# Issuing the DMAs of a hybrid layer's background sums from GpSimd instead of SyncE

## The chip, the cores and the metric

The kernel runs on one core of a Trainium2 chip, in one launch. The core has five engines with queues of their own: TensorE (PE: matmuls; PEld: its weight loads), VectorE (DVE), ScalarE (ACT), GpSimd (POOL) and SyncE (SP). Each queue is worked off in order, and an instruction that waits for a semaphore holds everything behind it on its engine. The metric is the device time of one execution in microseconds (us). A profiled execution gives the trace from which all rows below are taken.

## The reference, cut to what matters

The layer works on x with 2048 tokens and 1024 channels, in float32. Its first half (a state-space scan and a windowed attention, side by side) ends in x2, the residual stream. The second half is the MLP, with 4096 hidden channels:

```
x = x + rmsnorm(mix, norm_mix_post)                 # x2, 1024 x 2048
h = rmsnorm(x, norm_mlp_pre)
f = jnp.square(jax.nn.relu(h @ w_up)) @ w_down
x = x + rmsnorm(f, norm_mlp_post)
```

The row factor of the MLP's first rmsnorm is a scalar per token, so the kernel leaves it out of h and applies its square at the end (`drr` holds it); what enters the MLP is x2 times the weight vector.

## The kernel before

**The MLP's products.** `up` and `down_fast` use a seven-product scheme (Strassen's, in a form with running sums): a 2x2 block product is made with seven matmul products of sums and differences of blocks instead of eight. Each product needs a left factor made of blocks of weights and a right factor made of blocks of activations. Every factor is split into a high and a low part (fp32r), and three matmuls per k tile stand for one float32 product: 12 matmuls of 128x512 per product.

**Stages.** `main` runs the MLP's first layer for the token halves `hf` 0 and 1, each in 16 steps `p` (`up`), and then the second layer (`down_fast`, `down`). One step `p` is seven products in the order `PROD` = 1, 5, 6, 3, 7, 2, 4. Products share three PSUM banks (psmx, psmy, psmz), and a bank must be read before the next product adds to it: ACT copies products 1, 5 and 6 out (tiles c1, c5, c6; L1120) and reads product 4 with the relu (c4, L1073); DVE adds products 3, 7 and 2 to c6, c5, c1 (L1123). ACT then takes relu and square (L1073, L1074). The c tiles and sums of them (t1, t2, t4 on DVE, L1083 to L1095) are stored to DRAM as `dop` (L1079). The ring of c tiles has 5 buffers.

**Weights.** `up_weights` loads four blocks per step (`wu`, L982, 256 KB each, 8 buffers), forms sums on DVE (L964) and splits them (`wsplit`: ACT L969, DVE L970).

**Side work.** Generators (`side`) are stepped by a clock that counts matmul time, and a scheduler then places each engine's instructions by the time at which it expects them to be ready; only PE's order is kept as written. Around the change run:

- `sums` (from step `p` = 4 of the first half on): the background sums. 20 jobs. Jobs 0 to 3 load four blocks of x2 (L1158), scale them on DVE (L1167), form four differences on POOL (L1169 to L1172) and store seven tiles as `dxo` (L1185). Jobs 4 to 19 load four blocks of `w_down` (L1160), make four sums on POOL in place (L1179) and store them as `dws` (L1187). The four loaded tiles `sum` come from a ring of 4 buffers with the tag `nt`, which a job fills entirely; t1, t2, t4 come from rings of 3 and 2 buffers that `up` and the loads named stg use too.
- `r2`: the row factor of the rmsnorm, once per half at `p` = 8, for two token blocks. `rnorm` takes three tiles of the same `nt` ring (rn_v, rs_y, rs_t; ACT L282 and L284, DVE L283 to L288) and stores `drr` (L1338).
- `up_input1` (steps 14 and 15 of the first half): loads the 28 `dxo` tiles (`stage`, L199) and splits them (ACT L1012, DVE L1013) as the second half's right factors.
- `down_input` (steps 14 on of the second half as written; its first loads are placed some steps earlier): loads `dop` tiles (L199) and splits them (ACT L1246, DVE L1247).
- `down_weights`: its first four loads `wd` (L1218) use the `nt` ring again, after the last job's tiles. Later loads `wd` from `dws` (L1227) use another ring.

So in the kernel before, all of these loads and stores stand in SP's queue: weights, `dop`, stg, `drr`, and the background sums' 80 loads and 92 stores, each of 256 KB. The tiles of a job, and who gets the buffers next, tie POOL, SP, ACT and DVE together:

```
t = a[f"{i + 1}{k + 1}"] = self.nt("sum")
...
r = (x_sums if len(job) == 1 else w_sums)(*job, a)
...
raw = [self.nt("wd").rearrange("p (k c) -> p k c", k=4) for _ in range(2)]
```

Of the kernel before, what the change touches and what calls it, by code (L numbers as in the profile page):

```python
# [38 lines left out]
class Layer:  # L39
# [1105 lines left out]
    def sums(self):  # L1145


        nc = self.nc
        vec = self.vec["norm_mlp_pre"]

        def load(job):
            a = {}
            for i in range(2):
                for k in range(2):
                    t = a[f"{i + 1}{k + 1}"] = self.nt("sum")
                    if len(job) == 1:
                        kt = 4 * i + job[0]
                        nc.sync.dma_start(t, self.d_x2[kt, :, self.tok(1, k)])  # L1158
                    else:
                        nc.sync.dma_start(t.rearrange("p (k c) -> p k c", k=4),  # L1160
                                          self.a["w_down"][2 * job[1] + i, 2 * job[0] + k])
            return a

        def x_sums(i, a):
            for y in ("11", "12", "22", "21"):
                kt = 4 * int(y[0]) - 4 + i
                nc.vector.tensor_scalar(a[y], a[y], vec[:, kt:kt + 1], None, ALU.mult)  # L1167
            t1, t2, t4 = self.ld(name="t1"), self.gl("t2"), self.ld(name="t4")
            nc.gpsimd.tensor_sub(t1, a["12"], a["11"])  # L1169
            nc.gpsimd.tensor_sub(t2, a["22"], t1)  # L1170
            nc.gpsimd.tensor_sub(a["12"], a["22"], a["12"])
            nc.gpsimd.tensor_sub(t4, a["21"], t2)  # L1172
            return {1: a["11"], 3: a["22"], 2: a["21"], 5: t1, 6: t2, 7: a["12"], 4: t4}

        def w_sums(qt, p, a):
            r = {}
            for m, fn, x, y, o in ((5, "tensor_add", "21", "22", "21"), (6, "tensor_sub", "21", "11", "11"),
                                   (7, "tensor_sub", "22", "11", "22"), (3, "tensor_sub", "12", "11", "12")):
                getattr(nc.gpsimd, fn)(a[o], a[x], a[y])  # L1179
                r[m] = a[o]  # L1180
            return r

        def store(m, job, a):
            if len(job) == 1:
                nc.sync.dma_start(self.d_xo[m - 1, job[0]], a)  # L1185
            else:
                nc.sync.dma_start(self.d_ws[(5, 6, 7, 3).index(m), job[0], job[1]], a)  # L1187
        jobs = [(i,) for i in range(4)] + [(qt, p) for qt in range(4) for p in range(4)]
        for n, job in enumerate(jobs):
            a = load(job)  # L1190
            yield 10
            r = (x_sums if len(job) == 1 else w_sums)(*job, a)
            yield 8
            for m, t in r.items():
                store(m, job, t)
            if n == 3:
                self.flags.add("xo")
            elif n > 3 and job[1] == 3:
                self.flags.add(f"sum{job[0]}")
            yield 5  # L1200
# [462 lines left out]
```

## Time and profile before

| | us |
|---|---|
| median of 3 runs (3203.62 to 3218.38) | 3213.89 |
| the profiled execution, its own time | 3205.63 |
| its span in the trace | 3203.8 |
| PE busy in the span | 2949.0 (92%) |
| DVE busy | 2196.2 (69%) |
| ACT busy | 1554.0 (49%) |
| POOL busy | 903.7 (28%) |
| first background load issued / last background store issued | 1940.0 / 2465.2 |

PE is the engine that runs nearly all the time, and it is idle or slow only where one of the others is late. The background sums run from 1940 to 2470 us of the span. The rows of that stretch stand in the section after the next: busy time per stretch of time, the chain of waits, the timeline of single engines, the waits of SP's queue, and the groups of instructions of a line. A row of the timeline names in brackets how long the engine was idle before it and what ended that.

### The profile page before, as it was taken

The page shows a single profiled execution, that of the slowest core. Times are in us where ns is not written, and L with a number is a line of the kernel's source. Part 1 is how long each engine was busy: PE and PEld are TensorE (multiplying, and loading weights), DVE is VectorE, ACT ScalarE, POOL GpSimd, SP SyncE. Part 2 cuts the span into 40 slices and gives each one's busy share as a digit, 9 for nine tenths or more (in the row PEclk, how much of TensorE's full clock was granted, in tenths as well). Part 3 has the DMA queues.
Part 4 walks back from the last instruction along what each step waited for, and adds up shares of the span by engine and source line. Part 5 has one row for each costly group of instructions (what it writes and reads, how often), then busy time and mean ns, then how long its engine had stood idle before and what let it go on. Part 6 is the DMA issues. An engine that isn't in the chain of part 4 may idle for free. (4 is left out here: it accounts for less than half of the span.)

```text
span 3203.8 us, 41029 instructions
## 1 busy us (share of the span) xinstructions
PE 2949.0 (92%) x13560; PEld 2358.2 (74%) x13560; DVE 2196.2 (69%) x3671; ACT 1554.0 (49%) x2886; POOL 903.7 (28%) x743
## 2 busy tenths in 40 slices
PE   7989999989999899898897878998998999998996
PEld 6778887878886576576575657776887888877886
DVE  7355555547756778867868867677767567776765
ACT  4234566567765545322223354656565644454432
POOL 4242222112224344555545522141203000020001
PEclk9999999999999999899898989999999999999998
DMA  6767544465567755556436458778647565557633
GB/s 228 238 205 198 155 130 119 122 203 156 138 192 241 238 143 163 164 181 187 119 101 221 165 189 274 243 257 279 239 165 271 193 207 192 189 188 222 229 98 97
DMA packets 430213, 603.87 MB, mean 188 GB/s; under 512 B 35632, under 2 KB 203568, under 8 KB 430000
## 3 DMA queue, kind: packets, MB, share of 16 engines
q1 hardware_dynamic: 395376, 565.58, 57.0%
q10 hardware_dynamic: 34624, 35.66, 3.2%
q8 instruction: 108, 1.77, 0.2%
q14 instruction: 105, 0.86, 0.1%
HBM read 399.11 MB, written 201.99 MB: 188 GB/s over the span
## 5 line engine op out<-in xcount | busy, mean ns | idle before, releaser
L90 PE MATMUL psg<-h,ws 128*128 128x512 f32 x1920 | 486.6, 400 | 19.7 <-ACT z L474 17.9
L90 PEld LDWEIGHTS psg<-h,ws 128*128 128x128 f32 x1920 | 356.9, 190 | 93.4 <-issue 18.6
L88 PE MATMUL psmx<-b,ws 128*128 128x512 f32 x1152 | 297.0, 409 | 46.8 <-ACT c L1120 20.5
L222 POOL TENSOR_SCALAR ws<-wr 128x512 fp32r<-128x512 f32 x184 | 126.2, 686 | 755.9 <-PE psg L90 617.4
L88 PEld LDWEIGHTS psmx<-b,ws 128*128 128x128 f32 x1152 | 226.6, 198 | 102.3 <-ACT c L1120 22.4
L225 POOL TENSOR_TENSOR ws<-wr,ws 128x512 fp32r<-128x512 f32 x184 | 249.4, 1356 | 14.8
L90 PE MATMUL psg<-hr,ws 128*128 128x512 f32 x960 | 248.7, 400 | 4.0 <-DMA hr<-dh 3.3
L781 DVE CUSTOM_DVE_ANT_0 p<-psqk,pack,sinks 128x384 f32<-128x384 f32 (+1 forms) x256 | 151.9, 596 | 138.2 <-PE psqk L90 137.5
L90 PE MATMUL psg<-ga,ws 128*128 128x512 f32 x768 | 208.7, 424 | 28.9 <-DVE mix L897 14.2
L88 PE MATMUL psx<-ff,ws 128*128 128x512 f32 x1008 | 231.6, 390 | 0.0
L88 PEld LDWEIGHTS psx<-ff,ws 128*128 128x128 f32 x1008 | 189.2, 188 | 40.0 <-issue 0.5
L90 PE MATMUL psg<-ya,ws 128*128 128x512 f32 x768 | 213.0, 418 | 3.5 <-DVE ya L205 3.3
L969 ACT CAST ws<-wd 128x512 fp32r<-128x512 f32 x196 | 121.4, 622 | 177.6 <-PE psx L88 75.7
L90 PEld LDWEIGHTS psg<-ga,ws 128*128 128x128 f32 x768 | 149.4, 199 | 77.6 <-issue 13.6
L90 PEld LDWEIGHTS psg<-hr,ws 128*128 128x128 f32 x960 | 176.0, 189 | 40.8 <-DMA hr<-dh 6.1
L1179 POOL TENSOR_TENSOR sum<-sum 128x512 f32<-128x512 f32 x64 | 97.8, 1538 | 326.6 <-DMA sum<-w_down_dram 182.2
L90 PEld LDWEIGHTS psg<-ya,ws 128*128 128x128 f32 x768 | 142.0, 193 | 44.9 <-issue 15.1
L792 ACT ACTIVATE p<-p,m 128x384 f32<-128x384 f32 (+1 forms) x256 | 150.9, 591 | 37.4 <-DVE m L787 37.2
L90 PE MATMUL psy<-ff,ws 128*128 128x512 f32 x672 | 159.2, 394 | 7.2 <-DVE facc L1288 6.0
L210 ACT CAST pt<-pspt 128x512 fp32r<-128x512 f32 x184 | 107.0, 583 | 118.8 <-PE pspt L94 104.8
L970 DVE TENSOR_TENSOR ws<-wd,ws 128x512 fp32r<-128x512 f32 x196 | 137.7, 703 | 31.4 <-ACT ws L969 31.1
L211 DVE TENSOR_TENSOR pt<-pspt,pt 128x512 fp32r<-128x512 f32 x184 | 125.4, 683 | 49.2 <-ACT pt L210 48.8
(250 smaller groups left out, 6279.1 us busy)
## 6 DMA issues: line engine op xcount, KB each, us to landing
stg<-dop SPq DMA_DIRECT2D x196, 256.0 KB, 3.6
wu<-w_up_dram SPq DMA_DIRECT2D x128, 256.0 KB, 3.7
wr<-w_in_dram SPq DMA_DIRECT2D x120, 256.0 KB, 2.8
dop<-c SPq DMA_DIRECT2D x112, 256.0 KB, 3.4
wd<-dws SPq DMA_DIRECT2D x56, 512.0 KB, 4.2
k<-dk SPq DMA_DIRECT2D x56, 384.0 KB, 4.8
dop<-t SPq DMA_DIRECT2D x84, 256.0 KB, 3.5
wd<-w_down_dram SPq DMA_DIRECT2D x40, 512.0 KB, 4.7
```

The costliest lines, as they stand in the source:

```text
L88: self.nc.tensor.matmul(out, lhsT, rhs, start=False, stop=stop, skip_group_check=True)
L90: self.nc.tensor.matmul(out, lhsT, rhs, start=start, stop=stop)
L210: self.nc.scalar.copy(hi, src)
L211: self.nc.vector.tensor_sub(lo, src, hi.bitcast(F32))
L222: self.nc.gpsimd.tensor_scalar(w[:, 0], raw, 1.0, 0.0, ALU.mult, ALU.add)
L225: eng.tensor_sub(w[:, 1], raw, w[:, 0].bitcast(F32))
L781: nc.vector.tensor_tensor_reduce(out=p[:, :W], in0=ps[:, :W], in1=bias, scale=1.0, scalar=self.sinks[:, hd:hd + 1], op0=ALU.add, op1=ALU.m ...
L792: nc.scalar.activation(p4[r][:, :W], p4[r][:, :W], AF.Exp, bias=m[:, 0, r:r + 1], scale=float(np.float32(SLOPES[hd])), accum_out=m[:, 2, r ...
L969: self.nc.scalar.copy(w[:, 0], x)
L970: self.eng("wlo").tensor_sub(w[:, 1], x, w[:, 0].bitcast(F32))
L1179: getattr(nc.gpsimd, fn)(a[o], a[x], a[y])
```

## The change

The four `dma_start` calls of the background sums, two loads and two stores, are begun from GpSimd's queue. The tiles, the sums and their order in the program stay.

```
@@ load @@
-                        nc.sync.dma_start(t, self.d_x2[kt, :, self.tok(1, k)])
+                        nc.gpsimd.dma_start(t, self.d_x2[kt, :, self.tok(1, k)])
...
-                        nc.sync.dma_start(t.rearrange("p (k c) -> p k c", k=4),
+                        nc.gpsimd.dma_start(t.rearrange("p (k c) -> p k c", k=4),
                                           self.a["w_down"][2 * job[1] + i, 2 * job[0] + k])
@@ store @@
-                nc.sync.dma_start(self.d_xo[m - 1, job[0]], a)
+                nc.gpsimd.dma_start(self.d_xo[m - 1, job[0]], a)
...
-                nc.sync.dma_start(self.d_ws[(5, 6, 7, 3).index(m), job[0], job[1]], a)
+                nc.gpsimd.dma_start(self.d_ws[(5, 6, 7, 3).index(m), job[0], job[1]], a)
```

PE's order stays the same. On the other engines it moves, since the scheduler places the work anew. Five pieces follow; the numbers behind c and t name one buffer's use, so that a place can be found again.

POOL, one job of `w_down` in the changed kernel. Before, POOL's queue held in this stretch only the sums L1179, 64 in a row.

```order
L1160 DMA sum<-w_down_dram 128x512 x4
L1179 TENSOR_TENSOR sum<-sum 128x512 x2
L1187 DMA dws<-sum 128x512
L1179 TENSOR_TENSOR sum<-sum 128x512 x2
L1187 DMA dws<-sum 128x512 x3
```

The loads and stores of a job now stand between its sums, and the next job's loads behind its last store.

SP, steps 13 and 14 of the first half, where `up_input1` begins (dop is a store of `up`, wu a load of weights, stg<-dxo a load of `up_input1` further on); one piece of the difference.

```order
 L1079 DMA dop<-t_18716 128x512
-L982 DMA wu<-w_up_dram 128x512
-L1187 DMA dws<-sum 128x512 x3
-L982 DMA wu<-w_up_dram 128x512
-L1160 DMA sum<-w_down_dram 128x512 x4
+L982 DMA wu<-w_up_dram 128x512 x2
 L1079 DMA dop<-c_18746 128x512
 L982 DMA wu<-w_up_dram 128x512 x2
-L1187 DMA dws<-sum 128x512
 L1079 DMA dop<-c_18710 128x512
```

Eight instructions of the sums leave this place; what is left keeps its order.

SP, steps 11 and 12 of the second half, before the change (c_21080 and c_21054 are c5 and c1 of step 11; stg<-dop are the first loads of `down_input`).

```order
L1079 DMA dop<-c_21080 128x512
L982 DMA wu<-w_up_dram 128x512 x2
L1079 DMA dop<-c_21054 128x512
L1079 DMA dop<-t_21192 128x512
L1079 DMA dop<-t_21194 128x512
L1079 DMA dop<-c_21188 128x512
L1079 DMA dop<-c_21101 128x512
L1079 DMA dop<-t_21224 128x512
L1160 DMA sum<-w_down_dram 128x512 x4
L982 DMA wu<-w_up_dram 128x512
L199 DMA stg<-dop 128x512 x3
```

The last job's four loads stand ahead of the loads stg; the first load wd (L1218) stands 12 rows further on, behind the last stores dws.

The same place in the changed kernel.

```order
L1079 DMA dop<-c_21080 128x512
L982 DMA wu<-w_up_dram 128x512 x2
L1218 DMA wd<-w_down_dram 128x512
L1079 DMA dop<-c_21054 128x512
L1079 DMA dop<-t_21192 128x512
L1079 DMA dop<-t_21194 128x512
L1079 DMA dop<-c_21188 128x512
L1079 DMA dop<-c_21101 128x512
L1079 DMA dop<-t_21224 128x512
L199 DMA stg<-dop 128x512 x4
```

The four loads of the last job are gone from SP, and the first wd, whose buffer is that of the last job's first tile, has moved ahead of six stores dop and of the loads stg.

ACT, step 12 of the second half in the changed kernel (c_21218, c_21244 and c_21273 are c1, c5 and c6 of step 12).

```order
L1120 COPY c_21218<-psmx 128x512
L969 CAST ws<-wc 128x512
L1120 COPY c_21244<-psmy 128x512
L969 CAST ws<-wu 128x512
L1246 CAST ff<-stg 128x512 x2
L1120 COPY c_21273<-psmx 128x512
```

The first two casts of `down_input` now stand ahead of the copy of product 6; before, the first of them stood two rows behind it.

## Rows read from the trace of the kernel before

**Rows 1.** The page's busy time of two engines: us, share of span, instructions.
```profile
PE 2949.0 (92%) x13560; PEld 2358.2 (74%) x13560; DVE 2196.2 (69%) x3671; ACT 1554.0 (49%) x2886; POOL 903.7 (28%) x743
```
**Rows 2.** Stretches: length, PE, PEld, DVE, ACT, POOL busy (instructions), PEclk, DMA share, GB/s.
```profile
2080.00:2100.00 20.00, 20.00 (x90) 16.58 (x89) 15.30 (x17) 11.38 (x20) 11.73 (x8) 1.00 0.74 251
2140.00:2180.00 40.00, 30.17 (x123) 24.45 (x122) 19.26 (x30) 18.07 (x32) 10.54 (x8) 0.87 0.81 278
2180.00:2240.00 60.00, 54.85 (x223) 42.19 (x222) 49.63 (x72) 38.79 (x71) 7.89 (x5) 0.97 0.83 277
1980.00:2000.00 20.00, 17.07 (x68) 13.31 (x67) 13.74 (x22) 8.76 (x17) 2.05 (x2) 0.91 0.86 295
2060.00:2080.00 20.00, 16.91 (x68) 13.52 (x67) 13.34 (x21) 12.05 (x19) 5.10 (x4) 0.91 0.70 246
2440.00:2480.00 40.00, 31.52 (x132) 25.66 (x131) 24.71 (x29) 17.70 (x33) 12.14 (x8) 0.91 0.78 270
```
**Rows 3.** Chain of waits, 2155 to 2170 us: start us, duration us, engine, tile, line.
```profile
2155.60 4.56 DMA sum<-w_down_dram
...
2160.29 1.26 POOL sum L1179
...
2161.57 0.33 SPq L1187
...
2162.43 3.69 DMA stg<-dxo
...
2168.33 2.08 PE psmy L88 x4
```
**Rows 4.** Chain of waits, 2454 to 2474 us.
```profile
2454.39 0.44 SPq L1160
...
2455.35 5.34 DMA stg<-dop
...
2466.51 4.69 PE psmx L88 x12
2471.20 2.73 PE psmx L90 x12
```
**Rows 5.** SP queue's waits, 1900 to 2560 us: total us, times, longest us.
```profile
SPq L1187 <- POOL sum L1179: 68.9, 46, 3.2
```
**Rows 6.** L1160 (two rows), landing of L1187, L1179 (min/median/max); a cast on ACT.
```profile
L1160 SPq DMA_DIRECT2D sum<-w_down_dram x64: 327/422/1962, 2046.4 to 2454.4; - x64
DMA to landing us min/median/max: 2.6/4.2/5.9
...
DMA to landing us min/median/max: 2.0/2.1/4.9
...
L1179 POOL TENSOR_TENSOR sum<-sum x64: 1260/1622/1822, 2060.2 to 2463.5; 128x512 f32<-128x512 f32 x64
...
L969 ACT CAST ws<-wd 128x512 fp32r<-128x512 f32 x196 | 121.4, 622 | 177.6 <-PE psx L88 75.7
```
**Rows 7.** Timeline of POOL, four of the sixteen groups of four sums.
```profile
2081.84 6.07 POOL L1179 TENSOR_TENSOR sum<-sum 128x512 f32<-128x512 f32 x4 [16.37 <-DMA sum<-w_down_dram]
2094.02 6.83 POOL L1179 TENSOR_TENSOR sum<-sum 128x512 f32<-128x512 f32 x4 [6.11 <-DMA sum<-w_down_dram]
...
2408.13 6.93 POOL L1179 TENSOR_TENSOR sum<-sum 128x512 f32<-128x512 f32 x4 [114.98 <-DMA dop<-t]
2422.14 6.85 POOL L1179 TENSOR_TENSOR sum<-sum 128x512 f32<-128x512 f32 x4 [7.08 <-DMA sum<-w_down_dram]
```
**Rows 8.** Timeline of SP: the last store drr, and the store of c5 behind it.
```profile
2401.11 0.33 SPq L1338 DMA_DIRECT2D drr<-rs_y  x1
2401.84 0.33 SPq L1079 DMA_DIRECT2D dop<-c  x1
```
**Rows 9.** Timeline of ACT and of DVE: two waits for the sums' tiles.
```profile
2063.60 1.28 ACT L282 ACT_TABLE_LOAD   x1 [5.00 <-DMA dws<-sum]
...
1990.37 0.49 DVE L1167 TENSOR_SCALAR sum<-sum,vec 128x512 f32<-128x512 f32 x1 [4.91 <-DMA sum<-dx]
```

## The prediction

> **What bounds the kernel now.** The page's busy times come first: PE 92%, POOL 28% [rows 1]. POOL has room for more instructions; the time is PE's work plus the places where PE stands. The table of stretches then shows where PE stands while the background sums run. At full rate a group of 12 matmuls takes 2.73 us [rows 4], 0.227 us each, so 20 us hold about 88 and the undisturbed stretch shows 90 with those at its edges [rows 2]. By that count 2140 to 2180 us lost 54 matmuls (176 + 1 less 123), 12.2 us; 2180 to 2240 lost 43, 9.7 us; 1980 to 2000 and 2060 to 2080 lost 21 each, 4.8 us; 2440 to 2480 lost 45, 10.3 us [rows 2]. These 42 us, 1.3% of the time, are what any order of the queues could give back here.
>
> The chain of waits then tells who was late. Around 2160 us it runs from a load of `w_down` to the sum on POOL, to the store of that sum, which SP's queue held until POOL was done, then to the load stg behind it on SP, and so to ACT and to PE's restart at 2168.33 [rows 3]. That is one queue blocked at its head: SP waited 46 times, 68.9 us in all, for POOL's sums at the stores L1187 alone [rows 5], and whatever `up` needed next stood behind. Around 2455 the chain passes through the last job's loads and the load stg behind them, and PE restarts at 2466.51, its first 12 matmuls taking 4.69 us instead of 2.73 [rows 4]; the granted clock of such stretches is 0.87 to 0.91, part of them at the lower of its two levels [rows 2].
>
> **What the change removes.** SP loses 172 instructions and all waits for POOL's sums. Elsewhere this is hidden, since the weights are loaded a step ahead; it counts where the chain passes through SP: at the input phase, 2140 to 2240. There the load stg at 2162.43 stood behind a store that waited for a sum, and so for a load begun at 2155.60 [rows 3]; without it SP could have issued stg some 5 us sooner, and a dozen issues of 0.42 us [rows 6] go as well. Of the 22 us lost I take **10 us back**; bounds 4 (that one wait) and 18 (all but one landing of 3.69 us [rows 3], which the splits need anyway).
>
> **What it adds on POOL.** The trace before has no DMA issued by POOL. Its price c lies between SP's issue, 0.4 us, and POOL's own 128x512 instruction, 1.6 us [rows 6]; I take the middle, 1.0 us, since POOL has to do something for 128 rows but has no data to move. 172 of them are 172 us more on an engine with 28% busy [rows 1]: no bound by itself. What counts is the length of a job's chain, since POOL's queue now holds loads, sums and stores in one row. From the issue of its last load: 3.8 us to its landing (4.2 less the issue), two sums 3.1, a store c, two sums 3.1, three stores 3c, 1.7 until the last has landed (2.1 less the issue), and three loads 3c up to the next last load: **11.7 + 7c** [rows 6]. At c = 0.4 this gives 14.5, as the groups at 2408 and 2422 stand apart [rows 7]; at 1.0 it is 18.7, at 1.6 it is 22.9 us.
>
> The Trainium skill bears on c: "DMA: Bandwidth & Descriptors", section "Latency and other measured facts", gives the first byte of a DMA begun on GpSimd as about 1 us against about 0.6 us on the path of SyncE. As an estimate from it, a job's load and its store would each be 0.4 us later, 0.8 us a job, some 3 us over four jobs; no row here shows it, and it is left out of the sum.
>
> **Where POOL's pace reaches PE.** Three places.
>
> (a) *The first wd.* The last four jobs cannot start before `r2` frees the nt ring: its last store drr is issued at 2401.11 [rows 8] and lands 2.1 us later; two loads and a landing follow (2c + 3.8), so the first sums come at 2407 + 2c (2407.8 at SP's price; the trace has 2408.13 [rows 7]). The last job's first tile is free three job lengths and 6.2 + 2c + 1.7 later. Together T = 2407 + 2c + 3(11.7 + 7c) + 7.9 + 2c = 2450 + 25c: **2460, 2475, 2490** for the three prices. In SP's new order the first wd, which needs that buffer, stands behind c5 of step 11, and a step is 7 x 2.73 = 19.1 us; counted two steps on from c5 of step 9 at 2401.84 [rows 8], with two issues of wu, SP reaches it at about 2441. So SP stands there for 19 to 49 us, with six stores dop and the loads stg behind it. On ACT the first two casts of stg stand ahead of the copy of product 6, which PE needs before product 7. After T come seven issues on SP (3 us), the landing of stg (5.34 [rows 4]) and three ACT operations of 0.62 (1.9 us [rows 6]): PE starts product 7 at T + 10.2. Of the 10.3 us lost before, 2.0 are the slow restart and 8.3 the gap ahead of product 4, so product 7, two groups earlier, started at 2466.5 - 8.3 - 5.5 = 2452.7. The new stall is T - 2442.5; it takes the place of the old gap of 8.3, with the same slow restart. Net loss T - 2450.8: **9, 24 or 39 us**, and I take 24.
>
> (b) *The rmsnorm in the first half.* ACT waited 5.0 us at L282 for a store dws, until 2063.60 [rows 9], since rs_y takes the buffer of the sum just stored. On POOL that store stands behind the second sum and costs c, and the load ahead of it c: later by 2 to 4 us. PE waits behind it already, so **3 us lost**.
>
> (c) *The scaling of x2.* Jobs 0 to 3 have DVE between load and difference, in DVE's queue. Between the first scale of one job and the landing of the next one's last load POOL has seven stores, four loads, four sums of 1.6 and a landing of 3.8: 10.2 + 11c, so 15, 21 or 28 us [rows 6]. In the new order the second job's last scale stands 22 rows of DVE behind the first job's first, about as many as a step of 19 us holds, and its second scale some 3 us before that. At c = 1 that is some 4 us of stall and 2 of slow restart, and 2 more in the third job; the old wait of 4.91 us there [rows 9], worth 4.8 us of PE, goes. Net **3 us lost**; bounds a gain of 4 (c = 0.4, loads in time) and a loss of 12 (c = 1.6).
>
> Here a rule that speaks against the change can be weighed. DVE's operations in (a) are all TENSOR_TENSOR with two inputs; a scale L1167 has one and takes 0.49 us [rows 9], and 16 of them run. The Trainium skill, "SBUF — State Buffer", section "Who interferes with whom", says that DVE operations such as tensor_scalar can hold the port through which GpSimd writes its descriptors, for the whole instruction. By that (c) would be at most 16 x 0.49 = 8 us longer, the sum 28 us for 20, and (a) the same; no row before shows it.
>
> **The sum** at c = 1: 24 + 3 + 3 - 10 = 20 us slower. At 0.4: 9 + 2 - 4 - 10 = -3. At 1.6: 39 + 4 + 12 - 10 = 45. Against the profiled execution's own 3205.63 us that is 3226; the median lies 8.3 us above it, so **3234 us**.
>
> **The rivals.** *POOL issues as cheaply as SP* (c near 0.4): 3 us faster, 3211. For it: the job length at that price is what the trace shows [rows 7]. Against: it is one end of the bounds, and POOL's shortest 128x512 instruction takes 1.26 us [rows 6]. *Relief wins* (faster): the last four jobs run at the shortest distance seen, 12.2 us (2081.84 to 2094.02 [rows 7]), so T is 2407.8 + 37 + 8.7 = 2453 and the loss at (a) 3 us, while the input phase gives back 18 and (c) 4: 3 + 2 - 4 - 18 = -17, 3197. It decides from T below 2451. Against: that distance was reached with loads and stores on a queue beside POOL's. *Dear issue* (c = 1.6): 45 us slower, 3259. *No change*: SP's issue time was never on the path, and what is freed is needed by the landings anyway, while the last jobs' wait falls into a gap that exists already: within 5 us of 3214. For it: only 0.42 us an issue is saved, and the DMA engines are busy 70 to 86% of these stretches already [rows 2, 6]. The Trainium skill's rule in "DMA: Bandwidth & Descriptors", section "Issuing engines are not separate DMA queues", would end here: all engines' DMAs share the same 16 DMA engines, and a second issuer saves only issue time. The chain at 2160 speaks against it, since there SP waited for POOL and not for a transfer [rows 3]. That the DMAs stay on SP is excluded by the new order.
>
> **How the numbers follow.** Chances: forecast (c from 0.7 to 1.3, 12 to 33 us slower) 0.52; cheap issue 0.19; relief wins 0.10; dear issue 0.14; no change 0.05. The predicted time is the forecast's. The range leaves out the relief's far end and what is beyond 45 us: 3201 to 3257. A change of over 0.5% (16 us) is about what a measurement of this kernel can tell from none. Slower by that: the dear issue and three quarters of the forecast, 0.53. Faster: most of relief wins and a little of the cheap issue, 0.11. Within: 0.36.
>
> **What would show it.** Right: a stall of PE of over 15 us in steps 12 and 13 of the second half, SP's queue standing at L1218 with its longest wait there, a distance of 18 to 20 us between POOL's groups of four sums, and fewer lost matmuls in the input phase. Wrong: POOL's DMA under 0.5 us or over 1.6; SP passing L1218 without a wait; or ACT not standing at L1246.

## The result and the profile after

The changed kernel took 3260.65 us (median of 4 runs, 3249.91 to 3262.5) beside 3209.63 us for the kernel before (4 runs): a ratio of **1.0147, 95% interval 1.0125 to 1.0168**, so 40 to 54 us slower. The profiled execution took 3260.77 us. The forecast was slower, 3234 us, and its range ended at 3257. The sign was right; the size was not, and the term for the input phase had the wrong sign.

The page of the changed kernel first: busy times (us, share of the span, instructions), which answer to [rows 1].

```profile
PE 2965.8 (91%) x13560; PEld 2371.2 (73%) x13560; DVE 2205.1 (68%) x3671; ACT 1554.1 (48%) x2886; POOL 983.5 (30%) x915
```

Its two largest DMA queues on the page (packets, MB, share of 16 engines):

```profile
q1 hardware_dynamic: 370608, 520.48, 51.8%
q0 software_dynamic: 13760, 45.10, 4.2%
```

POOL has 172 instructions more and a queue of its own for 45 MB. Nothing in these lines says that it got slower; PE does the same 13560 matmuls. The price c of an issue on POOL stands in the views of the lines L1160 and L1187 (duration in ns, min/median/max; below each, issue to landing in us). They answer to [rows 6].

```profile
L1160 POOL DMA_DIRECT2D sum<-w_down_dram x64: 538/540/546, 2054.7 to 2492.4; - x64
DMA to landing us min/median/max: 2.8/5.9/7.4
...
L1187 POOL DMA_DIRECT2D dws<-sum x64: 542/553/573, 2074.7 to 2502.9; - x64
DMA to landing us min/median/max: 2.3/2.8/5.1
```

So c is 0.54 us, not the 1.0 that was taken; but a load lands after 5.9 us instead of 4.2, and a store after 2.8 instead of 2.1.

The stretches (length, PE, PEld, DVE, ACT, POOL busy with instructions, PEclk, DMA share, GB/s), which answer to [rows 2], show where PE lost time. What is lost moves every later place, by up to 50 us in the end.

```profile
1940.00:2000.00 60.00, 46.83 (x187) 37.53 (x186) 46.07 (x63) 26.56 (x47) 30.46 (x39) 0.89 0.77 266
2060.00:2100.00 40.00, 33.15 (x135) 26.67 (x134) 24.75 (x39) 20.23 (x34) 14.31 (x18) 0.91 0.62 207
2180.00:2240.00 60.00, 44.77 (x164) 35.32 (x165) 42.34 (x51) 28.49 (x52) 29.20 (x37) 0.83 0.79 271
2480.00:2520.00 40.00, 14.48 (x56) 11.52 (x55) 10.09 (x14) 8.24 (x15) 16.76 (x20) 0.66 0.60 202
```

The matmuls lost in a stretch are its length over 0.2267 us, plus 1, less its count; times 0.2267 that is the time. For the input phase both kernels are taken over the same 160 us, first the kernel before:

```profile
2140.00:2300.00 160.00, 145.02 (x610) 116.34 (x609) 117.24 (x157) 90.64 (x159) 42.02 (x28) 0.96 0.79 269
```

The changed kernel, the same stretch:

```profile
2140.00:2300.00 160.00, 130.70 (x514) 102.71 (x513) 118.02 (x139) 78.75 (x139) 76.16 (x95) 0.90 0.76 264
```

That is 21.9 us lost before and 43.7 after. By the same count 1940 to 2000 us (the scaling of x2) went from 10.4 to 17.8, 2060 to 2100 (the rmsnorm) from 4.9 to 9.6, and 2400 to 2540 (the first wd) from 11.7 to 29.4: 7 + 5 + 22 + 18 = 52 us more, of the 55 us between the two profiled executions. POOL's column shows what is new in the input phase: POOL is busy 76 us there, where it was 42, with 95 instructions for 28.

Such windows compare the same stretch of time and not the same work. PE's order is the same in both kernels, so one and the same matmul can be found in both traces. Here it is the first of a product ahead of the first scale of x2 (timeline of PE), in the kernel before:

```profile
1942.61 5.45 PE L88 MATMUL psmx<-b,ws 128*128 128x512 f32 x12 [5.37 <-DVE c L1123]
```

In the changed kernel:

```profile
1947.63 4.74 PE L88 MATMUL psmx<-b,ws 128*128 128x512 f32 x12 [5.88 <-DVE c L1123]
```

It starts 5 us later before the sums have done anything. By the same comparison the changed kernel lost 4 us from there to 2000 us of the kernel before, 4 from 2060 to 2100, 22 from 2140 to 2300 and 17 from 2400 to 2540: 47 us in one profile of each, as much as the ratio of the medians gives. So about 3 of the 7 us from 1940 to 2000 are that earlier gap, which lies whole inside the window only in the changed kernel.

The input phase falls into two parts by it. Three products in the kernel before (timeline of PE), the second behind the gap of [rows 3]:

```profile
2155.62 2.88 PE L88 MATMUL psmx<-b,ws 128*128 128x512 f32 x12
2168.33 5.26 PE L88 MATMUL psmy<-b,ws 128*128 128x512 f32 x12 [9.83 <-ACT c L1120]
...
2232.08 2.88 PE L90 MATMUL psmy<-b,ws 128*128 128x512 f32 x12
```

The same three in the changed kernel:

```profile
2171.75 3.04 PE L88 MATMUL psmx<-b,ws 128*128 128x512 f32 x12 [1.72 <-ACT c L1120]
2174.62 2.88 PE L88 MATMUL psmy<-b,ws 128*128 128x512 f32 x12
...
2268.07 2.88 PE L90 MATMUL psmy<-b,ws 128*128 128x512 f32 x12
```

They start 16.1, 6.3 and 36.0 us later. At the gap the changed kernel gained 9.8 us; behind it, it lost 29.7.

Two places of the changed kernel show the largest losses. At the first wd, the timeline of PE:

```profile
2514.05 4.86 PE L88 MATMUL psmx<-b,ws 128*128 128x512 f32 x12 [25.52 <-ACT c L1120]
```

The timeline of ACT there:

```profile
2512.24 1.27 ACT L1246 CAST ff<-stg 128x512 fp32r<-128x512 f32 x2 [28.00 <-DMA stg<-dop]
2513.42 0.58 ACT L1120 COPY c<-psmx 128x512 f32<-128x512 f32 x1
```

And the waits of SP's queue from 2440 to 2520 us (total us, times, longest):

```profile
SPq L1218 <- DMA sum<-w_down_dram: 19.6, 1, 19.6
...
SPq L1218 <- DMA dws<-sum: 5.5, 1, 5.5
```

PE's one gap of 25.52 us ends with ACT's copy, which stands behind the casts of stg, which SP could issue only after it had stood 25.1 us at L1218. The second place is the input phase: the timeline of DVE and POOL, single sums on DVE beside two pairs on POOL.

```profile
2227.20 3.12 DVE L1083 TENSOR_TENSOR t<-c,c 128x512 f32<-128x512 f32 x1
2227.26 2.50 POOL L1179 TENSOR_TENSOR sum<-sum 128x512 f32<-128x512 f32 x2
...
2245.87 3.11 DVE L1013 TENSOR_TENSOR b<-stg,b 128x512 fp32r<-128x512 f32 x1
2245.93 2.49 POOL L1179 TENSOR_TENSOR sum<-sum 128x512 f32<-128x512 f32 x2
```

A DVE sum of this size takes 0.69 us when POOL is quiet. Here it ends only after both of POOL's sums have ended.

### The profile page after: what moved, and what is told of

The parts are those of the page before. It is cut to its first block, busy times and chain, and to the rows that moved or that the text cites. A ratio compares the mean times of both kernels' runs of the same rounds, so it can differ in the third digit from the quotient of the medians.

```text
span 3258.9 us, 40975 instructions
## 1 busy us (share of the span) xinstructions
PE 2965.8 (91%) x13560; PEld 2371.2 (73%) x13560; DVE 2205.1 (68%) x3671; ACT 1554.1 (48%) x2886; POOL 983.5 (30%) x915
## 5 line engine op out<-in xcount | busy, mean ns | idle before, releaser
L90 PE MATMUL psg<-h,ws 128*128 128x512 f32 x1920 | 486.7, 400 | 19.4 <-ACT z L474 17.9
L225 POOL TENSOR_TENSOR ws<-wr,ws 128x512 fp32r<-128x512 f32 x184 | 249.8, 1358 | 14.7
L90 PEld LDWEIGHTS psg<-ga,ws 128*128 128x128 f32 x768 | 151.9, 203 | 75.4 <-issue 14.1
L1247 DVE TENSOR_TENSOR ff<-stg,ff 128x512 fp32r<-128x512 f32 x196 | 138.4, 723 | 39.1 <-ACT ff L1246 39.1
L1246 ACT CAST ff<-stg 128x512 fp32r<-128x512 f32 x196 | 119.5, 620 | 91.2 <-DMA stg<-dop 81.8
```

The source lines that it names most:

```text
L90: self.nc.tensor.matmul(out, lhsT, rhs, start=start, stop=stop)
L225: eng.tensor_sub(w[:, 1], raw, w[:, 0].bitcast(F32))
L1246: nc.scalar.copy(t[:, 0], x)
L1247: self.eng("flo").tensor_sub(t[:, 1], x, t[:, 0].bitcast(F32))
```

## The experiments

Two theories stood against each other for the input phase. **Theory 1, overlap:** in the kernel before, SP's order happened to keep most of the background sums out of the input phase; on a queue of their own they run right through it, and there they hold DVE (1a) or the loads (1b). **Theory 2, order:** the scheduler's new order of ACT and DVE costs it. All ratios are to the kernel before, on the same chip; intervals are 95%. The lost us are counted in the same four windows, from one profile each.

| kernel | median us | ratio (interval) | 1940-2000 | 2060-2100 | 2140-2300 | 2400-2540 |
|---|---|---|---|---|---|---|
| before | 3209.6 | 1 | 10.4 | 4.9 | 21.9 | 11.7 |
| after | 3260.65 | 1.0147 (1.0125-1.0168) | 17.8 | 9.6 | 43.7 | 29.4 |
| e1 loads only | 3290.54 | 1.0247 (1.0223-1.0272) | 16.5 | 8.7 | 64.3 | 22.6 |
| e2 stores only | 3254.13 | 1.0128 (1.0106-1.0150) | 17.2 | 6.0 | 43.0 | 19.2 |
| e3 wd too | 3238.95 | 1.0085 (1.0067-1.0104) | 14.7 | 9.6 | 41.9 | 2.2 |
| e4 first pause | 3242.02 | 1.0100 (1.0073-1.0126) | 15.3 | 10.3 | 30.1 | 18.0 |
| e5 no sums | 3211.40 | 0.9999 (0.9989-1.0009) | 16.5 | 4.2 | 17.9 | 10.1 |
| e7 hold | 3212.30 | 0.9996 (0.9982-1.0010) | 16.2 | 9.2 | 5.6 | 13.3 |
| e8 hold, wd | 3206.31 | 0.9982 (0.9969-0.9995) | 17.2 | 8.9 | 4.7 | 11.9 |
| e9 hold, wd, x on SP | 3194.70 | 0.9947 (0.9931-0.9964) | 8.1 | 8.9 | 4.7 | 1.7 |
| e10 memsets | 3208.96 | 1.0000 (0.9989-1.0010) | 17.8 | 3.0 | 23.3 | 7.8 |
| e12 before, hold | 3188.02 | 0.9933 (0.9917-0.9950) | 11.7 | 3.5 | 6.1 | 5.8 |
| e13 e12, wd | 3192.22 | 0.9934 (0.9910-0.9958) | 11.3 | 5.5 | 5.2 | 6.7 |

**e1, only the loads on GpSimd.**

```
-                nc.gpsimd.dma_start(self.d_xo[m - 1, job[0]], a)
+                nc.sync.dma_start(self.d_xo[m - 1, job[0]], a)
...
-                nc.gpsimd.dma_start(self.d_ws[(5, 6, 7, 3).index(m), job[0], job[1]], a)
+                nc.sync.dma_start(self.d_ws[(5, 6, 7, 3).index(m), job[0], job[1]], a)
```

> Only the loads of the background sums (L1158, L1160) are begun from GpSimd; their stores stay in SP's queue. Theory 1 (overlap: what costs time in the input phase is that the sums now run beside it): loads are no longer held by SP's order, so sums still run beside the input phase, and SP still stands at the stores L1185/L1187 for POOL's sums (69 us in the kernel before); both costs together, 30 to 55 us slower than the kernel before, with over 30 us of matmuls lost from 2140 to 2290 us. Theory 2 (order: the new order of ACT's and DVE's queues costs it, not the overlap): nothing about the sums' place matters, and the time lies halfway, 15 to 30 us slower than before. The stall of the first wd (L1218, 25 us of PE in the changed kernel) is smaller by 3c a job, about 5 us, by both.

Measured: 79 us slower (1.0247 beside 3211 us on that chip), more than either theory said, and 64.3 us lost in the input phase. SP's waits from 2130 to 2300 us:

```profile
SPq L1187 <- POOL sum L1179: 41.6, 25, 3.4
SPq L1187 <- DMA sum<-w_down_dram: 23.9, 5, 6.4
```

The loads run ahead on one queue while the stores that free their buffers stand in the other, so SP stands at the head of every job again, now inside the input phase. The longest gap of PE there is 22.08 us, from 2203 to 2225; SP got past L1187 only at 2214.7. The stg that PE's chain waited for went out at 2216.69, behind a load wu that had waited for DVE, and took 7.92 us to land. How much of the 64 us is SP's stand alone is not separated.

**e2, only the stores on GpSimd.**

```
-                        nc.gpsimd.dma_start(t, self.d_x2[kt, :, self.tok(1, k)])
+                        nc.sync.dma_start(t, self.d_x2[kt, :, self.tok(1, k)])
...
-                        nc.gpsimd.dma_start(t.rearrange("p (k c) -> p k c", k=4),
+                        nc.sync.dma_start(t.rearrange("p (k c) -> p k c", k=4),
```

> Only the stores of the background sums (L1185, L1187) are begun from GpSimd; their loads stay in SP's queue. Theory 1 (overlap): SP's order places the loads, and so the sums, where the kernel before has them, outside the input phase; SP no longer stands at the stores; the input phase loses 22 us of matmuls or less, as before, and the kernel takes 3195 to 3220 us, within 15 us of the kernel before. Theory 2 (order): the stores' move alone changes the order of ACT and DVE as the whole change does, and at least 15 of the 20 us lost more in the input phase stay: 3230 us or more. If SP stands at the next job's loads for POOL's stores instead, its longest waits are at L1160, 40 us or more in all.

Measured: 1.0128, a miss for theory 1 as it was put: loads in SP's queue are no guarantee that they stay out of the input phase. The scheduler's new order placed them in it. SP's largest wait from 2130 to 2300 us:

```profile
SPq L1160 <- DMA dws<-sum: 52.2, 20, 7.8
```

The stretch of the input phase:

```profile
2140.00:2300.00 160.00, 128.56 (x517) 101.73 (x518) 116.20 (x143) 78.20 (x139) 59.89 (x63) 0.90 0.80 273
```

POOL is busy 60 us there, and SP stands at L1160 for the stores of the job ahead, as the last sentence of the expectation said. The wait did not go when the stores went; it moved to the loads.

**e3, the first four wd on GpSimd as well.**

```
-                                nc.sync.dma_start(raw[x], self.a["w_down"][2 * (p + x), 0])
+                                nc.gpsimd.dma_start(raw[x], self.a["w_down"][2 * (p + x), 0])
```

> The changed kernel with one more move: the first four loads wd (L1218), which share the buffers of the sums, are begun from GpSimd too, so SP has nothing left that waits for those buffers. If SP's stand at L1218 (19.6 and 5.5 us) is what stops PE for 25.5 us before product 7 of step 12, that stop goes down to under 8 us and the time falls by 17 to 27 us against the changed kernel, to 3234 to 3244 us. Rival: PE waits there for the splits of wd, or for ACT behind DMAs that land late, whoever begins them; then the stop stays at over 15 us and the time within 6 us of the changed kernel's 3261. The input phase, 2140 to 2290 us, loses 42 us of matmuls in either case.

Measured: 3238.95 us, 22 us under the changed kernel, inside the range expected; the place loses 2.2 us instead of 29.4, and the input phase its 41.9 still. The row of PE at the same product, which stood for 25.52 us:

```profile
2491.71 3.02 PE L88 MATMUL psmx<-b,ws 128*128 128x512 f32 x12 [0.24 <-ACT c L1120]
```

SP's stand at L1218 is thus shown as the cause of that gap.

**e4, a pause that did not hold.** Ahead of the tenth job:

```
+            if n == 9:
+                yield self.until("B14")
+                g = self.cp.tile([P, 2], F32, tag="gate", name="gate")
+                nc.gpsimd.tensor_scalar(g, B[4][3][:, 1, 0:2].bitcast(F32), 1.0, None, ALU.mult)
```

> The changed kernel with a pause of the background sums: ahead of the tenth job POOL reads one element of the last gate tile, so that the jobs which ran beside the input phase come after it; every queue and the orders of ACT and DVE stay as they were but for this. Theory 1 (overlap): DVE's sums there fall back from about 3.1 us to 0.7 us where they stood beside POOL's, the loads stg from 6.2 us to about 4, and the matmuls lost from 2140 to 2290 us from 42 to 22 us or less: 3236 to 3246 us, 15 to 25 us faster than the changed kernel. Theory 2 (order): the same 42 us are lost without POOL, the time within 6 us of 3261 us. The stop at the first wd stays by both, and is up to 10 us longer if the later jobs push the last four.

Nothing that follows depends on the pausing instruction, so the scheduler let six jobs pass it: it ran at 2267.77, behind the last sums of the job before it (timeline of POOL):

```profile
2263.64 2.55 POOL L1179 TENSOR_TENSOR sum<-sum 128x512 f32<-128x512 f32 x2
...
2267.77 0.28 POOL L1193 TENSOR_SCALAR gate<-b 128x2 f32<-128x2 f32 x1
```

From 2140 to 2300 us seven jobs ran instead of eight, and the loss there fell by 14 us. This does not tell the two theories apart.

**e5, no sums of w_down on POOL.**

```
-                getattr(nc.gpsimd, fn)(a[o], a[x], a[y])
```

> The changed kernel without the additions and subtractions of the background sums of w_down on GpSimd (L1179; jobs 4 to 19): these sums are not computed, every load and store stays. A job is about 6 us shorter. By that alone the stop at the first wd (25.5 us before product 7 of step 12) falls by up to 18 us by every theory. The input phase, 2140 to 2290 us, tells apart why it loses 42 us of matmuls where the kernel before lost 22. Theory 1a (DVE is held while POOL's sums run): DVE's single sums of about 3.1 us are gone there, and it loses 25 us or less; 3222 to 3235 us in all. Theory 1b (the transfers compete for the DMA engines): the same bytes move in less time, the loads stg still land in 6 us or more, and it loses 35 us or more; 3240 to 3250 us in all.

Measured: 3211.40 us, below what 1a gave; 17.9 us lost in the input phase. But the jobs, with no sums, were through by 2200 us, so the transfers were gone early too: this pointed to 1a without excluding 1b. e10 was made for that.

**e7, a hold that holds.** The tile to be loaded is written first, so the load has to wait:

```
+            hold = job == (1, 1)
...
                     t = a[f"{i + 1}{k + 1}"] = self.nt("sum")
+                    if hold:
+                        nc.gpsimd.tensor_scalar(t[:, 0:2], B[4][3][:, 1, 0:2].bitcast(F32), 1.0, None, ALU.mult)
...
         for n, job in enumerate(jobs):
+            if n == 9:
+                yield self.until("B14")
```

> The changed kernel with the background sums held out of the input phase for certain: ahead of each of the four loads of the tenth job POOL writes two elements into the tile to be loaded, computed from the last tile b of the input phase, so the load has to wait for it (in the first attempt the pausing instruction was moved behind six further jobs). Theory 1 (overlap of sums with the input phase): 2140 to 2290 us loses 22 us of matmuls or less instead of 42, DVE's sums of 3.1 us and the loads stg of 6.2 us are gone there. Theory 2 (the new order of SP, ACT and DVE, not the overlap): 35 us or more are lost still. The eleven held jobs need about 17 us each and come late in the second half: the stop at the first wd may grow by 10 to 40 us, so the total says little, 3235 to 3270 us.

Measured: 3212.30 us, 48 us below the changed kernel and below the 3235 to 3270 expected. The stretch:

```profile
2140.00:2300.00 160.00, 156.51 (x682) 127.15 (x681) 122.02 (x175) 100.54 (x176) 50.02 (x64) 1.00 0.76 256
```

DVE's splits of the loads stg, 2140 to 2290 us (busy us, mean ns | idle before), in the changed kernel:

```profile
L1013 DVE TENSOR_TENSOR b<-stg,b 128x512 fp32r<-128x512 f32 x28 | 28.2, 1031 | 27.7 <-ACT b L1012 27.7
```

The same group with the hold:

```profile
L1013 DVE TENSOR_TENSOR b<-stg,b 128x512 fp32r<-128x512 f32 x28 | 18.8, 689 | 8.8 <-ACT b L1012 8.6
```

The loss fell from 43.7 to 5.6 us, and the mean split from 1031 to 689 ns. Theory 1 stands; theory 2 falls for the most part, since loads and stores stand in the changed kernel's queues still; what the scheduler reordered around the held jobs was not separated. The hold gains more than the change had cost there: the kernel before lost 16 us more than e7 does. It did not lose them in the same way: its splits took 0.69 us and its loads stg landed in 3.9 us, as with the hold. By the same matmuls 12 of the 16 us lay at the one gap of [rows 3] and the slow restart behind it.

**e8 and e9, the hold with wd, and with x on SP.** e8 is e7 with the edit of e3; e9 is e8 with the loads L1158 and the stores L1185 back on `nc.sync`.

> The hold of the run before and the first four loads wd (L1218) from GpSimd as well. If both costs of the changed kernel are what was said (overlap with the input phase 20 us and more, SP's stand at L1218 some 22 us), both go, and 3205 to 3225 us are left. If the held jobs make the sums late for the down product, PE stands before step 12 or 13 for them, and the time is 3240 us or more.

> The run before, with the loads and stores of the first four jobs (the sums of x, L1158 and L1185) back in SP's queue. If the 7 us that the changed kernel lost from 1940 to 2000 us come from POOL's queue placing these loads and stores, they return: 3198 to 3218 us, 5 to 9 us below the run before it. If they come from elsewhere (the drift of that stretch from run to run), the two agree within 4 us.

e8 took 3206.31 us, inside its range. It gained 6 us on e7, not the 22 of e3; why is not shown, but with jobs held back the buffers come at other times. e9 took 3194.70: 12 us below e8 and below its range. All versions with any x load or store on POOL lost 15 to 18 us from 1940 to 2000 us, the three with all of them on SP beside the kernel before 8 to 12. Counted by the same matmuls, from 1944 to 2000 us of the kernel before, the first lost 3.0 to 8.2 us more than that kernel, the three between a gain of 0.3 and a loss of 2.2. So a loss of about 4 us there belongs to POOL's queue; the rest of e9's 12 us does not come from this stretch.

**e10, memsets for sums.**

```
-                getattr(nc.gpsimd, fn)(a[o], a[x], a[y])
+                for _ in range(3):
+                    nc.gpsimd.memset(a[o], 1.0)
```

> The changed kernel, with each addition or subtraction of the background sums of w_down on GpSimd (L1179, 128x512, 1.3 us) replaced by three memsets of the same tile, which read nothing from SBUF: these sums are not computed, every load and store stays, and POOL stays busy between them. Theory 1a (DVE is held while POOL reads SBUF for its sums): DVE's single sums of 3.1 us are gone, and 2140 to 2300 us loses 25 us of matmuls or less instead of 45, though the loads stg still land in 5.5 us or more. Theory 1b (the transfers compete for the DMA engines, at the same number of bytes): 35 us or more are lost there still. If both count, it is between. The total goes with it: 3225 to 3245 us by 1a, 3250 us or more by 1b, less what shorter jobs save at the first wd.

Measured: 3208.96 us, below what 1a gave. The stretch:

```profile
2140.00:2300.00 160.00, 145.26 (x604) 116.46 (x604) 102.92 (x159) 90.21 (x158) 69.88 (x140) 0.96 0.80 276
```

POOL's memsets and DVE's splits, 2140 to 2290 us:

```profile
L1180 POOL MEMSET sum<- 128x512 f32 x84 | 40.4, 520 | 20.4 <-DMA sum<-w_down_dram 20.2
...
L1013 DVE TENSOR_TENSOR b<-stg,b 128x512 fp32r<-128x512 f32 x28 | 19.0, 690 | 23.1 <-ACT b L1012 23.1
```

The issues of stg there (KB each, median us to landing):

```profile
stg<-dxo SPq DMA_DIRECT2D x28, 256.0 KB, 5.7
```

POOL is nearly as busy as in the changed kernel, the jobs follow each other a little faster (every 14 to 18 us, there 17 to 19), and stg lands nearly as late (5.7 us for 6.2; 3.9 in the kernel before). Yet every group of DVE's 128x512 sums has a mean of 0.69 us, and the loss is 23.3 us instead of 43.7. So of the changed kernel's 43.7 us some **20 come from POOL's sums holding DVE (1a)**. That is nearly all of the 22 us net that the change added here to the 21.9 of the kernel before. With the hold 5.6 us are left, so another 18 go when the jobs go. That these are due to **the transfers beside the input phase (1b)** is argued from stg's later landing and not shown: no run took the transfers out and left the sums in place. The split also takes the two as additive, which no run shows.

**e12, the hold in the kernel before.** The edit of e7, on the kernel before.

> The kernel before, all loads and stores in SP's queue, with the background sums held out of the input phase by the same four instructions ahead of the tenth job. Theory A (what the held versions gain is the hold alone, and GpSimd's queue is worth nothing by itself): 2140 to 2300 us loses 8 us or less, as with the hold in the changed kernel, and the time is 3190 to 3203 us, below the 3212 us of the changed kernel with the hold. Theory B (a hold needs a queue of its own: in SP's queue the held loads stand in front of the loads and stores of the up projection): SP stands at L1160 for POOL's hold, or the eleven later jobs block SP at L1187 in the second half as they did before, and the time is 3212 us or more.

Measured: **3188.02 us, 0.9933 (0.9917 to 0.9950)**, faster than both kernels and than e7 and e8, the held versions with the sums of x on GpSimd's queue; e9's interval overlaps with its own. It agrees with theory A, at 2 us below its range. The stretch:

```profile
2140.00:2300.00 160.00, 156.36 (x680) 126.84 (x679) 125.29 (x174) 99.19 (x173) 32.43 (x24) 1.00 0.77 262
```

SP's largest wait from 2130 to 2300 us:

```profile
SPq L1190 <- POOL sum L1182: 24.4, 19, 3.1
```

(L1190 and L1182 are L1187 and L1179 of the kernel before.) SP still stands 24 us for POOL's sums, and only 6 us of PE are lost. The same 160 us in two parts, the first with all 28 loads stg (2150.7 to 2207.4), the second with five jobs:

```profile
2140.00:2215.00 75.00, 71.36 (x305) 56.45 (x304) 59.70 (x94) 53.36 (x95) 1.51 (x3) 1.00 0.74 250
2215.00:2300.00 85.00, 85.00 (x376) 70.38 (x375) 65.59 (x81) 45.83 (x79) 30.92 (x22) 1.00 0.79 273
```

In the second part POOL's sums run and SP stands for them, and PE loses nothing: the wait that the prediction wanted to remove costs nothing once the sums lie where PE has its operands. In the kernel before SP stood 12 us at the stores L1187 just ahead of the first load stg (2140 to 2162 us), and PE's gap of 9.83 us followed. Here the first stg is issued at 2150.7 with no such wait, and the gap is gone.

**e13, e12 with wd on GpSimd**, the edit of e3.

> The kernel before with the hold, and the first four loads wd (L1218 in the kernel before) begun from GpSimd. In the kernel before with the hold SP waits little at these loads, and 6 us of PE are lost around them (from 2440 to 2460 us). If moving these four is worth something by itself, those 6 us go: 3180 to 3184 us against 3188. If their place only matters where the sums' own loads and stores run on GpSimd's queue, as in the changed kernel, where SP stood 25 us there, the time is the same within 4 us.

The ratio is 0.9934 beside 0.9933: the same. With the sums' own loads and stores on SP it makes no difference here who begins wd.

## Why the prediction was right in its sign and wrong in its size

**The input phase: the step that failed.** The prediction took 10 us back there, bounds 4 and 18; 22 us more were lost. It read [rows 3] rightly: SP did stand behind POOL, and without this wait stg came sooner. The gap at 2168.33 is gone in the changed kernel, a gain of 9.8 us. What failed is that the sum took this relief for the whole effect on the input phase. It had no term for what the freed sums do beside the rest of it, and there 30 us were lost. The same rows hold this reading too: a background sum and its load stood in the input phase at all. Its own row in [rows 2], 2180 to 2240 us, had POOL at 7.89 us busy of 60: the order of SP's queue, where their loads had their turn, kept the sums out (the order and not the queue by itself, as e2 shows). What was freed ran into the stretch with the least room for it: POOL 29.20 us of 60 in the changed kernel. e7 and e12 show that the place of the sums decides. e10 shows through what most of it goes: POOL's sums hold DVE's, 20 us. The loads' later landing had no term either.

**The price c.** Taken as 1.0, measured 0.54; "cheap issue" (c near 0.4) was nearer. At 0.54, read between its three prices, the prediction's own terms give some 3 us slower, 3216 us. The distance of jobs was not 11.7 + 7c = 15.5 us for it but 17.0 to 19.3 from 2149 to 2280 us and 17.1, 18.1 and 14.1 at the end (timeline of POOL, the first pair of each of the last four jobs):

```profile
2446.94 2.66 POOL L1179 TENSOR_TENSOR sum<-sum 128x512 f32<-128x512 f32 x2 [5.79 <-DMA sum<-w_down_dram]
...
2464.01 3.06 POOL L1179 TENSOR_TENSOR sum<-sum 128x512 f32<-128x512 f32 x2 [6.57 <-DMA sum<-w_down_dram]
...
2482.12 2.98 POOL L1179 TENSOR_TENSOR sum<-sum 128x512 f32<-128x512 f32 x2 [6.07 <-DMA sum<-w_down_dram]
...
2496.21 2.60 POOL L1179 TENSOR_TENSOR sum<-sum 128x512 f32<-128x512 f32 x2 [3.29 <-DMA sum<-w_down_dram]
```

These answer to [rows 7]. The terms that were too small are the landings, of a load 5.9 us where 4.2 was used and of a store 2.8 where 2.1 was. The errors nearly cancel in the input phase and in part at the end: 18.7 had been forecast. Two figures of the prediction do not follow from its own sum: c = 0.7 gives about 9 us slower and not 12, and 45 us slower is 3259, so that the range's end at 3257 was 2 us short of what it was meant to hold.

**(a) The first wd: right in mechanism and place, and by luck nearly in size.** drr was issued at 2437.08 in the changed kernel, 36 us later than in [rows 8], from what was lost ahead of it. T moved along and with c = 0.54 is 2437.1 + 48.9 + 13.5 = 2499.5; the first wd went at 2501.1. PE restarted 12.9 us after that, where 10.2 had been worked out. The net loss is 18 us (11.7 to 29.4; 17 by the same matmuls), where 24 had been taken from bounds of 9 and 39, and e3 removes it. At the measured c the formula gives 13, so that 24 came near is in part luck.

**(b) The rmsnorm** lost 5 us more, 3 were said. e5 and e10, whose jobs on POOL are other than in the changed kernel by the sums alone, bring it back to 4.2 and 3.0. Their first store dws was issued at 2059.5 and 2065.0 us, in the changed kernel only at 2074.7, behind four loads and two sums: it is that store's place on POOL, as said. **(c) The scaling** lost 7 us more in the window and 4 by the same matmuls, 3 were said; e9 gives it back. Here a wait of DVE on late loads was named. PE's waits for DVE from 1940 to 2000 us grew from 5.4 to 13.2 us (c of L1123); 5.9 of these are the gap ahead of the first scale, the other 7.3 follow waits of DVE at L1167 (timeline of DVE in the changed kernel):

```profile
1971.89 0.49 DVE L1167 TENSOR_SCALAR sum<-sum,vec 128x512 f32<-128x512 f32 x1 [5.12 <-issue]
...
1993.44 0.49 DVE L1167 TENSOR_SCALAR sum<-sum,vec 128x512 f32<-128x512 f32 x1 [4.16 <-DMA sum<-dx]
```

The second row names the load; what the first waited for the profile does not show. So (a), (b) and (c) together cost 30 us by the windows and 25 by the same matmuls, where 24 + 3 + 3 were forecast: the sum of the losses was nearly right, by errors that cancelled in part, and the gain of 10 came at its place and was outweighed.

**The rivals.** "Relief wins" fell: the input phase gave back 10 us of its 18 at one gap and lost 30 behind it. "Dear issue", 3259 us, came out nearest, but for another reason than its price, so it was not borne out. "No change" fell: the Trainium skill's rule ("DMA: Bandwidth & Descriptors", "Issuing engines are not separate DMA queues"), that a second issuer saves only issue time, has nothing against it in these traces as to bandwidth (269 and 264 GB/s in the input phase), but the second queue made the kernel 47 us slower through what now runs beside what, and that is not issue time. The rule that was weighed in (c), a lock of DVE's tensor_scalar on GpSimd's descriptors, at most 8 us, is hardly tested: no load L1158 was issued beside a scale L1167. Eight stores L1185 were; six took 0.54 to 0.56 us on POOL, as elsewhere, the other two 0.62 and 0.82, some 0.4 us more in all.

What mattered stands in the section that was quoted there for another rule. The trace shows DVE's two-input sums at 0.69 us beside memsets on POOL, and at 3.12 beside a pair of POOL's sums. The Trainium skill, "SBUF — State Buffer", "Who interferes with whom", says it so: a DVE instruction with two inputs in SBUF contends with a GpSimd instruction that reads SBUF, not with one that only writes. e10 agrees on both halves.

**What would show it.** A stall of over 15 us before product 7 of step 12, SP's longest wait at L1218, and ACT at L1246 all came. Fewer lost matmuls in the input phase did not, nor did 18 to 20 us between the last jobs except once; in the input phase most distances lay there.

## What to carry to other kernels

A queue that blocks is also a brake: before freeing a stream of background work from it, find the stretch into which that work will now run, and who has no slack there; then price the neighbours (sums that hold another engine's, slower landings), not only the issue. Here placing the work (e12, 0.67% faster on the old queue) was worth more than the choice of queue (1.47% slower without the placing; with it, e7, 0.9996, no difference from the kernel before, and slower than e12). And a second in-order queue can move a wait instead of removing it: e1 and e2 each left SP standing at the other half of the pair.

## What was not expected of the hardware

Beside a group of four sums on POOL in a row, the kernel before shows DVE's sums and POOL's taking turns. In the changed kernel a store's issue splits the group into pairs. Beside the first pair turns are taken still. Beside the second pair, in the eleven cases from 2095 to 2290 us, the DVE sum that met it ended only after both of POOL's, whether it started ahead of the pair or inside its first sum (at 2283.64 us, 2.57 us long). The timeline of POOL and DVE in the kernel before:

```profile
2180.66 6.76 POOL L1179 TENSOR_TENSOR sum<-sum 128x512 f32<-128x512 f32 x4 [15.21 <-DMA sum<-w_down_dram]
2181.15 1.72 DVE L1083 TENSOR_TENSOR t<-c,c 128x512 f32<-128x512 f32 x1
2182.90 1.67 DVE L1086 TENSOR_TENSOR t<-c,t 128x512 f32<-128x512 f32 x1
```

There each side takes about 1.7 us a sum (POOL 6.76 for four); in the pair at 2227.26 POOL takes 1.25 a sum and DVE 3.12. Why the turns stop there is open; no run tried it. A DMA issue on POOL took 0.54 us with little spread, and its landing at the least 2.8 us against 2.6 from SP for loads, 2.3 against 2.0 for stores [rows 6].
